# Output operands of the next token group split one tile per step, first norm in half-row steps

## The chip, the cores and the metric

The kernel runs on one core of one Trainium2 chip. The metric is the device time of one execution in microseconds (us), as the median of three runs. The engines are TensorE (PE in the profile), VectorE (DVE), ScalarE (ACT), GpSimd (POOL) and SyncE (SP), which issues the DMA transfers.

## The reference, cut to what matters

One layer of a decoder trunk on 2048 tokens of width 1024, in float32. One projection feeds two groups of heads, four recurrent ones (hgrn) and eight of stick-breaking attention. Their outputs are normalised, projected, normalised again and added to the residual; then come a feed-forward block (FFN) and a gated embedding.

```python
u = rmsnorm(h, attn_pre_norm[i])
proj = u @ w_in[i]
hq, hf, hi, hg, sq, sk, sv = jnp.split(proj, splits, axis=-1)
o_hg = rmsnorm(hgrn2_mix(hq, hf, hi, lb), hg_out_norm[i]) * silu(hg)
o_sb = rmsnorm(stick_breaking_mix(sq, sk, sv), sb_out_norm[i])
mix = jnp.concatenate([o_hg, o_sb], axis=-1) @ w_out[i]
h = h + rmsnorm(mix, attn_post_norm[i])
u = rmsnorm(h, ffn_pre_norm[i])
gate, up = jnp.split(u @ w_gate_up[i], [D_FF], axis=-1)
h = h + rmsnorm((silu(gate) * up) @ w_down[i], ffn_post_norm[i])
...
```

The change concerns `mix` (the output projection), the two norms behind it, and what is prepared for them.

## The kernel before, in words

**Tiling.** The 2048 tokens are cut into four groups of 512 (`NG`, `GT`), a group into four row blocks of 128 (`TT`), and the width of 1024 into eight blocks of 128 (`ND`); `HH` is 4, so tiles 0 to 3 of a group's output belong to the hgrn heads and tiles 4 to 7 to attention. Every product of two float32 tiles is made by three matmuls of a high and a low part (`mm3`, lines 217 to 219), so each operand is split first: ScalarE casts the high part (line 203), GpSimd or VectorE subtracts it for the low part (line 204). A weight is loaded and split in the same way by `weight`; of split weights three stand at a time.

**Stages.** In projection, attention and hgrn recurrence are woven together up to about 1144 us. Then the output projections of the four groups follow, `out_proj(0)` to `out_proj(3)`, at 1144 to 1244, 1244 to 1345, 1345 to 1405 and 1405 to 1460 us; attention and hgrn of the last group still run beside the first two. Behind them stand the FFN and the embedding, to 3011 us.

**What the change touches.** `out_load(g)` loads the eight output tiles of a group from `o_s` (line 627, tile `tmp`, two buffers), splits tiles 0 to 3 by lines 203 and 204, scales and splits tiles 4 to 7 by lines 631 (ScalarE) and 632 (VectorE), and sums the squares of the latter in `oss` (lines 636 and 638 on ScalarE, 639 on GpSimd). The split operands are called `uh` and `ul`; their pool holds two groups (`UB`). `out_proj(g)` first turns `oss` into the row scales `rg` (lines 653 to 656), then runs four quarters of the output columns, each in two parts, with the results in `mix` (lines 682 and 684). `post_mix(g)` is run beside the following `out_proj`: for each row block `t` it loads the residual `h`, computes the scale of the row (`row_rstd`: a sum of squares on ScalarE, line 267, and two small GpSimd instructions, lines 269 and 272), multiplies `mix` (line 708, VectorE, two halves), adds it to `h` (line 709, first half on VectorE, second half on GpSimd), computes the scale of the new row and writes the normalised row `un_s` (line 713, ScalarE).

**What sets the order.** `weave(main, slots, subs)` steps the main stream and deals out the steps of the others in proportion; `Stream` wraps a generator, `drain` runs it to its end. PE runs in the order in which the program is written. On VectorE, ScalarE, GpSimd and SyncE a scheduler with a time model of its own puts the instructions in order while the program is built, starting from the order in which they are written; on the chip each engine then runs its own list strictly in that order. The VectorE and GpSimd lists hold attention's work too: line 458 is the low part of an attention operand, line 441 its scan, line 445 a product behind the scan, line 572 a product of the recurrence. `t_first` and `turn` prepare the FFN's first operands (lines 822 and 823: `uh`, `wh`, `wl` of a tile `wr`).

In the program before, `out_load(g + 1)` is written in one piece ahead of `out_proj(g)` (for the last group, ahead of `out_proj(2)`; for group 0, ahead of the last projection stretch, `n == 6`), and `post_mix` yields once for each row block.

## Time and profile before

| | us |
|---|---|
| median of three runs | 3013.46 (3012.3, 3013.46, 3015.99) |
| the profiled execution | 3012.98 |
| its span on the core | 3010.8 |
| PE busy | 2915.9 (97%) |
| VectorE busy | 2088.6 (69%) |
| ScalarE busy | 1576.9 (52%) |
| GpSimd busy | 1437.9 (48%) |
| out_proj(0) to out_proj(3) | 1144 to 1460 |

The profile comes from one execution; the span runs from its first to its last record. The shares are means over stages that differ much. Beside them the trace has, for any stretch of the span, the busy time of each engine and the granted TensorE clock as a share of full speed, the list of an engine's instructions in time, and the idle times of an engine with what ended them. In a row of a timeline the bracket gives the idle time ahead of the instruction and the instruction that released it.

### The profile page before, as it was taken

How to read it: one execution, taken by the hardware profiler on the slowest of the kernel's cores; microseconds unless marked ns; L12 is line 12 of the kernel's file. 1: busy time of each engine (PE TensorE's matmuls, PEld its weight loads, DVE VectorE, ACT ScalarE, POOL GpSimd, SP SyncE). 2: the span in 40 equal slices, each digit the busy share in tenths (PEclk: the TensorE clock that was granted, in tenths of full speed). 3: DMA queues.
4: the chain of work that ended last, by engine and by line, in shares of the span. 5: the costliest groups of instructions: out<-in, count | busy, mean ns of one | idle time of the engine just before them, and what ended most of it. 6: DMA issues, size and time to landing. Idle time of an engine off the chain costs nothing. (4 is left out here: it accounts for less than half of the span.)

```text
span 3010.8 us, 52896 instructions
## 1 busy us (share of the span) xinstructions
PE 2915.9 (97%) x18316; PEld 2423.5 (80%) x18316; DVE 2088.6 (69%) x2953; ACT 1576.9 (52%) x3180; POOL 1437.9 (48%) x1398
## 2 busy tenths in 40 slices
PE   8999999999999999898899999999999999999999
PEld 7888788878787888788777778888888888878777
DVE  3555666677777776756788787755787776656685
ACT  5666756666667666667523233445433323545542
POOL 3344455545556666855523222445723231446653
PEclk9999999999999999999999999999999999999999
DMA  7775665455445444557867677667965555677974
GB/s 220 217 215 152 180 181 164 146 171 164 139 138 163 148 132 140 162 182 268 277 219 246 222 263 244 213 191 224 334 204 168 175 173 174 207 217 226 333 249 160
DMA packets 469419, 602.28 MB, mean 200 GB/s; under 512 B 43168, under 2 KB 277664, under 8 KB 469152
## 3 DMA queue, kind: packets, MB, share of 16 engines
q1 hardware_dynamic: 469152, 598.91, 63.6%
q8 instruction: 144, 2.36, 0.3%
q14 instruction: 123, 1.01, 0.1%
HBM read 439.89 MB, written 158.86 MB: 199 GB/s over the span
## 5 line engine op out<-in xcount | busy, mean ns | idle before, releaser
L822 ACT CAST wh<-wr 128x512 fp32r<-128x512 f32 x600 | 351.8, 618 | 459.4 <-PE mm L218 187.2
L823 POOL TENSOR_TENSOR wl<-wr,wh 128x512 fp32r<-128x512 f32 x256 | 372.3, 1460 | 453.0 <-ACT wh L822 426.7
L445 POOL TENSOR_TENSOR a<-be,ring 128x512 f32<-128x512 f32 (+2 forms) x320 | 318.8, 997 | 415.2 <-DVE ring L441 390.1
L217 PE MATMUL mm<-uh,wh 128*128 128x512 f32 x1168 | 484.4, 415 | 7.2 <-DVE c L830 2.2
L219 PE MATMUL mm<-uh,wl 128*128 128x512 f32 x1168 | 460.7, 394 | 2.3 <-DVE wl L823 2.3
L218 PE MATMUL mm<-ul,wh 128*128 128x512 f32 x1168 | 459.2, 393 | 0.0
L823 DVE TENSOR_TENSOR wl<-wr,wh 128x512 fp32r<-128x512 f32 x344 | 297.7, 873 | 167.4 <-ACT wh L822 160.7
L441 DVE TENSOR_TENSOR_SCAN ring<-z,ring,be 128x512 f32<-128x512 f32 x192 | 245.7, 1280 | 105.5 <-ACT z L427 102.5
L217 PE MATMUL mm<-wh,uh 128*128 128x256 f32 (+1 forms) x992 | 306.5, 309 | 0.1
L218 PE MATMUL mm<-wl,uh 128*128 128x256 f32 (+1 forms) x992 | 291.6, 294 | 0.8 <-POOL wl L823 0.8
L219 PE MATMUL mm<-wh,ul 128*128 128x256 f32 (+1 forms) x992 | 291.6, 294 | 0.0
L219 PEld LDWEIGHTS mm<-uh,wl 128*128 128x128 f32 x1168 | 220.4, 189 | 53.5 <-DVE wl L823 2.7
L217 PEld LDWEIGHTS mm<-uh,wh 128*128 128x128 f32 x1168 | 221.6, 190 | 51.3 <-issue 3.3
L218 PEld LDWEIGHTS mm<-ul,wh 128*128 128x128 f32 x1168 | 221.7, 190 | 39.9 <-DVE ul L823 0.5
L458 DVE TENSOR_TENSOR al<-tr,ah 128x512 fp32r<-128x512 f32 (+1 forms) x320 | 192.1, 600 | 84.5 <-ACT ah L456 83.8
L203 ACT CAST wh<-wr 128x512 fp32r<-128x512 f32 x288 | 178.1, 619 | 132.7 <-PE mm L218 75.0
L204 POOL TENSOR_TENSOR wl<-wr,wh 128x512 fp32r<-128x512 f32 x144 | 190.1, 1320 | 102.8 <-ACT wh L203 92.1
L823 POOL TENSOR_TENSOR wl<-s,wh 128x512 fp32r<-128x512 f32 x44 | 95.5, 2175 | 274.0 <-ACT wh L822 255.5
L456 ACT CAST ah<-tr 128x512 fp32r<-128x512 f32 (+1 forms) x320 | 167.7, 524 | 106.4 <-PE tr L453 102.8
L426 ACT ACTIVATE be<-z 128x512 f32<-128x512 f32 (+2 forms) x320 | 171.1, 535 | 87.0 <-PE z L424 36.9
L217 PEld LDWEIGHTS mm<-wh,uh 128*128 128x128 f32 x992 | 189.5, 191 | 8.1 <-issue 0.3
L218 PEld LDWEIGHTS mm<-wl,uh 128*128 128x128 f32 x992 | 189.8, 191 | 6.3 <-POOL wl L823 1.2
(317 smaller groups left out, 7261.8 us busy)
## 6 DMA issues: line engine op xcount, KB each, us to landing
wr<-in_w_gate_up_dram SPq DMA_DIRECT2D x308, 256.0 KB, 3.9
wr<-in_w_in_dram SPq DMA_DIRECT2D x224, 256.0 KB, 3.1
wr<-hid_s SPq DMA_DIRECT2D x154, 256.0 KB, 3.0
wr<-in_w_down_dram SPq DMA_DIRECT2D x110, 256.0 KB, 3.4
wr<-wd_s SPq DMA_DIRECT2D x88, 256.0 KB, 3.2
kt<-k_s SPq DMA_DIRECT2D x80, 256.0 KB, 3.1
vt<-v_s SPq DMA_DIRECT2D x80, 256.0 KB, 3.3
wr<-h_s SPq DMA_DIRECT2D x80, 256.0 KB, 4.1
```

What stands on the lines that cost most here:

```text
L203: nc.scalar.copy(hi, src)
L204: (lo_engine or nc.gpsimd).tensor_tensor(lo, src, hi.bitcast(F32), op=ALU.subtract)
L217: nc.tensor.matmul(o, l[0], r[0], start=start, stop=False)
L218: nc.tensor.matmul(o, l[0], r[1], start=False, stop=False)
L219: nc.tensor.matmul(o, l[1], r[0], start=False, stop=stop)
L426: nc.scalar.activation(be[:, :n], z[:, :n], AF.Sigmoid, scale=0.125)
L441: nc.vector.tensor_tensor_scan(r[:, o:o + n][:, ::-1], z[:, :n][:, ::-1], be[:, :n][:, ::-1], init, op0=ALU.mult, op1=ALU.bypass)
L445: nc.gpsimd.tensor_tensor(a[:, :n], be[:, :n], r[:, o + 1:o + n + 1], op=ALU.mult)
L456: nc.scalar.copy(hi[:, lo_c:], tr[:, lo_c:])
L458: nc.vector.tensor_tensor(lo[:, lo_c:], tr[:, lo_c:], hi[:, lo_c:].bitcast(F32), op=ALU.subtract)
L822: nc.scalar.copy(hi, src)
L823: lo_engine.tensor_tensor(lo, src, hi.bitcast(F32), op=ALU.subtract)
```

## The change

`out_load` becomes a generator of nine steps: the first loads tile 0, each further one loads the next tile and splits the one at hand. It is dealt out over the slots of the preceding stream: for group 0 over the second half of the last projection stretch, for group 1 over `out_proj(0)`, for groups 2 and 3 over `out_proj(1)` and `out_proj(2)`. `post_mix` becomes eight steps of half a row: the loads and the first scale of a row (`ready`) are written one row ahead, the normalised row (`normed`) one step late. No arithmetic is changed and no instruction is added or taken away.

```diff
--- before.py
+++ after.py
@@ -619,12 +619,20 @@
     HG_STEPS = HH * 11 + 2
 
 
+    def o_raw(g, i):
+        r = tmp()
+        nc.sync.dma_start(r, o_s[g][i])
+        return r
+
     def out_load(g, res):
+
         ops = []
         acc = None
+        nxt = o_raw(g, 0)
+        yield
         for i in range(ND):
-            raw = tmp()
-            nc.sync.dma_start(raw, o_s[g][i])
+            raw = nxt
+            nxt = o_raw(g, i + 1) if i + 1 < ND else None
             if i >= HH:
                 hi, lo = operand(wpool, "u", UB)
                 gs = g_sb[:, i - HH:i - HH + 1]
@@ -639,7 +647,9 @@
                     nc.gpsimd.tensor_tensor(acc, acc, raw, op=ALU.add)
             else:
                 ops.append(split(wpool, "u", UB, raw))
-        res["o"], res["oss"] = ops, acc
+            if i == ND - 1:
+                res["o"], res["oss"] = ops, acc
+            yield
 
     def out_proj(g, res):
         ops, acc = res["o"], res["oss"]
@@ -698,21 +708,36 @@
         gb = [xt("gb") for _ in range(2)]
         for j in range(2):
             nc.sync.dma_start(gb[j], attn_post_norm[0:1][:, j * GT:(j + 1) * GT].to_broadcast((P, GT)))
-        for t in range(TT):
+
+        def ready(t):
             hs = [xt("h"), xt("h")]
             for j in range(2):
                 nc.sync.dma_start(hs[j], x[g * GT + t * P:g * GT + (t + 1) * P, j * GT:(j + 1) * GT])
-            r = row_rstd(mix[t])
+            return hs, row_rstd(mix[t])
+
+        def normed(t, hs, r):
+            for j in range(2):
+                nc.scalar.activation(mix[t][j], hs[j], AF.Copy, scale=r)
+                nc.sync.dma_start(un_s[g][t * P:(t + 1) * P, j * GT:(j + 1) * GT], mix[t][j])
+
+        nxt = ready(0)
+        late = None
+        for t in range(TT):
+            hs, r = nxt
             for j in range(2):
                 d = mix[t][j]
                 nc.vector.scalar_tensor_tensor(d, d, r, gb[j], op0=ALU.mult, op1=ALU.mult)
                 (nc.gpsimd if j else nc.vector).tensor_tensor(hs[j], hs[j], d, op=ALU.add)
                 nc.sync.dma_start(h_s[g][t * P:(t + 1) * P, j * GT:(j + 1) * GT], hs[j])
-            r = row_rstd(hs)
-            for j in range(2):
-                nc.scalar.activation(mix[t][j], hs[j], AF.Copy, scale=r)
-                nc.sync.dma_start(un_s[g][t * P:(t + 1) * P, j * GT:(j + 1) * GT], mix[t][j])
-            yield
+                if j == 0:
+                    if late is not None:
+                        normed(*late)
+                else:
+                    nxt = ready(t + 1) if t + 1 < TT else None
+                    late = (t, hs, row_rstd(hs))
+                    if t + 1 == TT:
+                        normed(*late)
+                yield
 
     def post_late(g):
 
@@ -1239,8 +1264,14 @@
         nxt = g + 2 if kind == "b" and g + 2 < NG else None
         toks = in_norm(nxt) if nxt else []
         if n == 6:
-            out_load(0, res[0])
-        weave(main, slots - tail, ra.part(slots - tail), rh.part(slots - tail, 1 if hg_n < slots else None))
+            ol = Stream(out_load(0, res[0]))
+        if n == 6:
+            part = slots // 2
+            weave(main, slots - part, ra.part(slots - part), rh.part(slots - part, 1 if hg_n < slots else None))
+            weave(main, part, ra.part(part), rh.part(part, 1 if hg_n < slots else None), (ol, ND + 1, 0))
+            ol.drain()
+        else:
+            weave(main, slots - tail, ra.part(slots - tail), rh.part(slots - tail, 1 if hg_n < slots else None))
         if n in (3, 5):
             hg.drain()
         if nxt:
@@ -1263,26 +1294,25 @@
                 yield
 
     for g in range(NG - 1):
-        if g + 1 < NG - 1:
-            out_load(g + 1, res[g + 1])
+        ol = Stream(out_load(g + 1, res[g + 1]))
         op = Stream(out_proj(g, res[g]))
         if g == 0:
             weave(op, 2, rates.part(2), r2.part(2))
             hgs[2].drain()
-            weave(op, OP_SLOTS - 2, rates.part(OP_SLOTS - 2), r3.part(OP_SLOTS - 2))
+            weave(op, OP_SLOTS - 2, rates.part(OP_SLOTS - 2), r3.part(OP_SLOTS - 2), (ol, ND + 1, 0))
         elif g == 1:
-            weave(op, half, rates.part(half), r3.part(half), (pm, TT, 0))
+            weave(op, half, rates.part(half), r3.part(half), (pm, 2 * TT, 0), (ol, 4, 1))
             tu = Stream(turn(un_s[0], u_s[0], g_ffn, ["mm"], xt, ev))
-            weave(op, half, rates.part(half), r3.part(half), (tu, 9, 0))
+            weave(op, half, rates.part(half), r3.part(half), (tu, 9, 0), (ol, 5, 1))
             hgs[3].drain()
             att_stream.drain()
             side.close()
             big[0] = ctx.enter_context(tc.tile_pool(name="bigr", bufs=1, side="right"))
             mm_tags[:] = ["mm", "z", "mm", "z", "mm", "av"]
         else:
-            out_load(NG - 1, res[NG - 1])
-            weave(op, half, (pm, TT, 0))
+            weave(op, half, (pm, 2 * TT, 0), (ol, ND + 1, 1))
             weave(op, half, (Stream(first_operands()), ND, 1))
+        ol.drain()
         op.drain()
         pm = Stream(post_mix(g, res[g]["mix"]))
 
@@ -1291,7 +1321,7 @@
     drive.prepare(2)
     op = Stream(out_proj(NG - 1, res[NG - 1]))
     tu = Stream(turn(un_s[1], u_s[1], g_ffn, ["tr", "hg"], xt, ev))
-    weave(op, half + 2, (pm, TT, 0), (tu, 9, 0))
+    weave(op, half + 2, (pm, 2 * TT, 0), (tu, 9, 0))
 
     def third_operands():
         for k in range(ND // 2):
```

PE's list is the same in both programs. The other lists move less than the diff suggests, since the scheduler had already spread the burst: tiles 0 to 5 of each `out_load` stand about where they stood. Two places where the lists differ follow, on two engines each. The numbers behind names count tiles in the program and differ from before to after.

**VectorE, early in out_proj(1).** `mix`, `rstd2`, `gb` and `h` belong to `post_mix(0)`, `ul<-tmp` is a tile of group 2's operands, `al` an attention operand. Before:

```order
L441 SCALAR_TENSOR_TENSOR ring3_204<-z_16649,be_16653 128x512
L653 COPY rg_18230<-hgss_181 128x4
L632 SCALAR_TENSOR_TENSOR ul_16636<-tmp_16633,g_sb_572,uh_16635 128x512
L458 TENSOR_TENSOR al_16669<-tr_16662,ah_16667 128x512
L632 SCALAR_TENSOR_TENSOR ul_16644<-tmp_16641,g_sb_572,uh_16643 128x512
L654 COPY rg_16721<-tr_16716 128x4
L608 TENSOR_TENSOR gate_16040<-hg_16552,gate_16040 128x512
L708 SCALAR_TENSOR_TENSOR mix_15294<-mix_15294,rstd2_16935,gb_16684 128x512
L708 SCALAR_TENSOR_TENSOR mix_15948<-mix_15948,rstd2_16935,gb_16685 128x512
```

After:

```order
L441 SCALAR_TENSOR_TENSOR ring3_204<-z_16593,be_16597 128x512
L729 SCALAR_TENSOR_TENSOR mix_15238<-mix_15238,rstd2_16803,gb_16628 128x512
L729 SCALAR_TENSOR_TENSOR mix_15918<-mix_15918,rstd2_16803,gb_16629 128x512
L730 TENSOR_TENSOR h_16794<-h_16794,mix_15238 128x512
L458 TENSOR_TENSOR al_16613<-tr_16606,ah_16611 128x512
L664 COPY rg_16651<-tr_16646 128x4
L608 TENSOR_TENSOR gate_16010<-hg_16552,gate_16010 128x512
L729 SCALAR_TENSOR_TENSOR mix_15239<-mix_15239,rstd2_17001,gb_16628 128x512
L729 SCALAR_TENSOR_TENSOR mix_15919<-mix_15919,rstd2_17001,gb_16629 128x512
L730 TENSOR_TENSOR h_16992<-h_16992,mix_15239 128x512
```

The two operand tiles (line 632, now line 640) are gone from here, and rows 1 and 2 of the norm (line 729, formerly 708) stand on both sides of `al`.

**GpSimd, behind that.** `qp` is the recurrence's product for which PE waits, `rg` the row scales of `out_proj(1)`. Before:

```order
L655 TENSOR_SCALAR rg_16721<-rg_16721 128x8
L639 TENSOR_TENSOR oss_16623<-oss_16623,tmp_16641 128x512
L709 TENSOR_TENSOR h_16927<-h_16927,mix_15948 128x512
L656 TENSOR_TENSOR rg_16721<-rg_16721,neghalf_168 128x8
L445 TENSOR_TENSOR a_16766<-be_16762,ring0_198 128x512
L572 TENSOR_TENSOR qp_16778<-qp_16778,pd_16776 128x256
```

After:

```order
L665 TENSOR_SCALAR rg_16651<-rg_16651 128x8
L269 TENSOR_SCALAR ssum_17006<-ss_17003 128x1
L269 TENSOR_SCALAR ssum_17195<-ss_17192 128x1
L730 TENSOR_TENSOR h_16993<-h_16993,mix_15919 128x512
L666 TENSOR_TENSOR rg_16651<-rg_16651,neghalf_168 128x8
L272 TENSOR_TENSOR rstd2_17008<-ssum_17006,neghalf_168 128x1
L272 TENSOR_TENSOR rstd2_17197<-ssum_17195,neghalf_168 128x1
L445 TENSOR_TENSOR a_16696<-be_16692,ring0_198 128x512
L572 TENSOR_TENSOR qp_16708<-qp_16708,pd_16706 128x256
```

The operand tile (line 639) has left, and the scales of further rows (lines 269 and 272) stand ahead of `qp`.

**ScalarE, in out_proj(2).** `wh<-wr` by line 203 is a weight of the output projection, `uh<-wr` by line 822 (now 847) an FFN operand, `junk` a sum of squares. Before:

```order
L203 CAST wh_18429<-wr_18427 128x512
L822 CAST uh_18618<-wr_18616 128x512
L822 CAST uh_18651<-wr_18649 128x512
L267 ACTIVATE junk_191,ss_18322<-h_18305 128x512
L822 CAST uh_18696<-wr_18694 128x512
L822 CAST uh_18729<-wr_18727 128x512
L682 ACTIVATE mix_18238<-mm_18278,rg_18230 128x256
L631 ACTIVATE uh_18187<-tmp_18185,g_sb_572 128x512
L267 ACTIVATE junk_191,ss_18322<-h_18306 128x512
L203 CAST wh_18435<-wr_18433 128x512
```

After:

```order
L203 CAST wh_18385<-wr_18383 128x512
L847 CAST uh_18651<-wr_18649 128x512
L267 ACTIVATE junk_191,ss_18437<-mix_16659 128x512
L847 CAST uh_18696<-wr_18694 128x512
L847 CAST uh_18729<-wr_18727 128x512
L847 CAST uh_18774<-wr_18772 128x512
L720 ACTIVATE mix_16657<-h_18219,rstd2_18341 128x512
L720 ACTIVATE mix_17492<-h_18220,rstd2_18341 128x512
L847 CAST uh_18807<-wr_18805 128x512
L203 CAST wh_18391<-wr_18389 128x512
```

Between the two weights stand five FFN operands and a normalised row (line 720) now, where four FFN operands, an evacuation (line 682) and an operand tile (line 631) stood.

**GpSimd, a little later in out_proj(2).** Before:

```order
L204 TENSOR_TENSOR wl_18436<-wr_18433,wh_18435 128x512
L639 TENSOR_TENSOR oss_18167<-oss_18167,tmp_18185 128x512
L269 TENSOR_SCALAR ssum_18406<-ss_18403 128x1
L272 TENSOR_TENSOR rstd2_18408<-ssum_18406,neghalf_168 128x1
L709 TENSOR_TENSOR h_18400<-h_18400,mix_17529 128x512
L204 TENSOR_TENSOR wl_18530<-wr_18527,wh_18529 128x512
```

After:

```order
L204 TENSOR_TENSOR wl_18392<-wr_18389,wh_18391 128x512
L269 TENSOR_SCALAR ssum_18440<-ss_18437 128x1
L272 TENSOR_TENSOR rstd2_18442<-ssum_18440,neghalf_168 128x1
L647 TENSOR_TENSOR oss_18414<-oss_18414,tmp_18408 128x512
L730 TENSOR_TENSOR h_18434<-h_18434,mix_17494 128x512
L269 TENSOR_SCALAR ssum_18447<-ss_18444 128x1
L848 TENSOR_TENSOR wl_18908<-wr_18903,wh_18907 128x512
L204 TENSOR_TENSOR wl_18502<-wr_18499,wh_18501 128x512
```

The norm's add of row 3 (line 730) and one FFN split (line 848) have come ahead of the weight's low part `wl_18502` (before, `wl_18530`).

## Rows read from the trace of the kernel before

**Rows 1.** The page's first part: busy time of each engine over the span.

```profile
PE 2915.9 (97%) x18316; PEld 2423.5 (80%) x18316; DVE 2088.6 (69%) x2953; ACT 1576.9 (52%) x3180; POOL 1437.9 (48%) x1398
```

**Rows 2.** Waits of PE, 929 to 960 us: place, total us, times, longest.

```profile
PE hg L535 <- POOL qp L572: 0.8, 1, 0.8
```

**Rows 3.** Waits of PE, 1144 to 1244 us.

```profile
PE av L470 <- DVE al L458: 4.8, 1, 4.8
```

**Rows 4.** Waits of PE, 1244 to 1345 us.

```profile
PE hg L535 <- POOL qp L572: 5.1, 3, 2.6
PE av L470 <- DVE al L458: 2.3, 1, 2.3
...
PE hg L535 <- DVE small L538: 1.1, 1, 1.1
PE av L469 <- ACT ah L456: 1.0, 1, 1.0
```

**Rows 5.** Waits of PE, 1345 to 1405 us.

```profile
PE z L218 <- POOL wl L204: 8.4, 4, 4.2
```

**Rows 6.** Waits of PE, 1405 to 1460 us.

```profile
PE z L218 <- POOL wl L204: 0.9, 2, 0.5
```

**Rows 7.** Windows: span, busy (count) PE, PEld, DVE, ACT, POOL, clock, DMA share, GB/s.

```profile
1091.00:1105.00 14.00, 14.00 (x137) 11.53 (x136) 9.83 (x15) 9.78 (x23) 11.86 (x17) 1.00 0.58 189
...
1197.00:1207.00 10.00, 10.00 (x161) 8.70 (x160) 6.65 (x10) 6.72 (x14) 5.71 (x11) 1.00 0.44 135
...
1244.00:1268.00 24.00, 17.81 (x272) 15.71 (x272) 18.10 (x25) 15.46 (x36) 22.68 (x25) 0.99 0.64 205
...
1238.00:1245.00 7.00, 5.52 (x27) 5.34 (x27) 5.25 (x8) 4.80 (x12) 6.00 (x11) 0.52 0.42 151
1275.00:1282.00 7.00, 4.95 (x34) 4.52 (x35) 5.63 (x7) 3.46 (x12) 4.99 (x6) 0.53 0.54 187
1357.00:1364.00 7.00, 3.54 (x16) 3.54 (x17) 6.43 (x7) 4.84 (x11) 6.19 (x5) 0.52 1.02 339
```

**Rows 8.** Instructions on the tile tmp: form, count, min/median/max ns.

```profile
L632 DVE SCALAR_TENSOR_TENSOR ul<-tmp,g_sb,uh x16: 724/751/1783, 939.4 to 1365.2; 128x512 fp32r<-128x512 f32 x16
...
L639 POOL TENSOR_TENSOR oss<-oss,tmp x12: 1258/1304/1749, 946.2 to 1367.8; 128x512 f32<-128x512 f32 x12
```

**Rows 9.** Instructions of line 708: min/median/max ns.

```profile
L708 DVE SCALAR_TENSOR_TENSOR mix<-mix,rstd,gb x24: 737/752/1779, 1233.6 to 1434.2; 128x512 f32<-128x512 f32 x24
```

**Rows 10.** Timeline of VectorE, 1231.5 to 1241 us: start, us, instruction [idle <- releaser].

```profile
1233.57 2.77 DVE L708 SCALAR_TENSOR_TENSOR mix<-mix,rstd,gb 128x512 f32<-128x512 f32 x2 [0.47 <-POOL rstd L272]
1236.26 0.88 DVE L632 SCALAR_TENSOR_TENSOR ul<-tmp,g_sb,uh 128x512 fp32r<-128x512 f32 x1
...
1238.75 0.68 DVE L458 TENSOR_TENSOR al<-tr,ah 128x512 fp32r<-128x512 f32 x1
```

**Rows 11.** Timeline of GpSimd, 1247 to 1268 us.

```profile
1254.20 1.84 POOL L656 TENSOR_TENSOR rg<-rg,neghalf 128x8 f32<-128x8 f32 x1
...
1257.07 0.83 POOL L572 TENSOR_TENSOR qp<-qp,pd 128x256 f32<-128x256 f32 x1
...
1260.87 1.01 POOL L272 TENSOR_TENSOR rstd<-ssum,neghalf 128x1 f32<-128x1 f32 x1
```

**Rows 12.** Timeline of VectorE, 1272 to 1279 us.

```profile
1273.58 2.62 DVE L708 SCALAR_TENSOR_TENSOR mix<-mix,rstd,gb 128x512 f32<-128x512 f32 x2
```

**Rows 13.** Timeline of ScalarE, 1349 to 1370 us.

```profile
1357.13 1.15 ACT L822 CAST uh<-wr 128x512 fp32r<-128x512 f32 x2
...
1365.13 0.62 ACT L203 CAST wh<-wr 128x512 fp32r<-128x512 f32 x1 [3.04 <-PE mm L219]
```

**Rows 14.** Timeline of GpSimd, 1345 to 1392 us.

```profile
1357.08 1.65 POOL L709 TENSOR_TENSOR h<-h,mix 128x512 f32<-128x512 f32 x1 [1.29 <-DVE mix L708]
...
1372.25 1.68 POOL L709 TENSOR_TENSOR h<-h,mix 128x512 f32<-128x512 f32 x1 [1.60 <-DVE mix L708]
...
1375.56 3.45 POOL L823 TENSOR_TENSOR wl<-wr,wh 128x512 fp32r<-128x512 f32 x2
```

## The prediction

> **What bounds the kernel now.** I read the share of busy time first: PE is busy for 2915.9 of 3010.8 us, and the next engine, VectorE, for 69% of the span [rows 1]. So PE sets the time, its list is the same in both programs, and the change can only move PE's idle time and the clock that it is granted. All of PE's idle time is about 95 us (3010.8 less 2915.9). Next I read the list of PE's waits, stretch by stretch, where the moved instructions stand. Around the end of the projections there is one wait of 0.8 us, for GpSimd [rows 2]; beside out_proj(0) and (1) attention waits 4.8 us for one low part `al` and later 2.3, and the recurrence 5.1 us in three pieces for `qp` [rows 3, 4]; in out_proj(2) PE waits four times, 8.4 us together, for the low part of a weight [rows 5]; in out_proj(3) 0.9 us [rows 6]. That is 22.3 us, with smaller ones of 1.1 and 1.0 [rows 4] some 24 us, and it is all that this change can reach directly. Third come the windows: in three of seven microseconds each, at 1238, 1275 and 1357 us, the granted clock is 0.52 or 0.53, the lower of the two levels [rows 7]. Each stands right behind one of the long waits (the 4.8 us for the `al` of 1238.75 [rows 10], the 2.3 us for the next late one, and the longest of the four for weights, 4.2 us). In the three, PE is busy for 5.52, 4.95 and 3.54 us; at full clock the same matmuls would take half, so a slow stretch costs 2.8, 2.5 and 1.8 us. Direct waits and slow stretches together: about 31 us, 1% of the time. A gain above that is excluded.
>
> **The change part by part.** The sum is made against the profiled execution, 3012.98 us, which lies 0.5 under the median of 3013.46.
>
> *Operand tiles.* Comparing the lists, tiles 0 to 5 of each group stay about where they were. Tiles 6 and 7 (per group two loads, five ScalarE, two VectorE and three GpSimd instructions, GpSimd's `oss` add of tile 5 among them) go to a later place. One VectorE instruction is 0.75 us, one GpSimd add 1.30 [rows 8], so 1.5 and 3.9 us of work leave one place and come to another.
>
> - Group 0: they leave 945 to 959 us, where a 0.8 us wait of PE [rows 2] stands with GpSimd's add next to it, and come to 1091 to 1105, where PE is busy for all of 14.00 us, and GpSimd for 11.86 [rows 7]. There 2.1 us of GpSimd are free, 1.8 less than the 3.9 that come; out_proj(0) needs them only at 1144, so the cover is the rest of that stretch. I take -0.7; without the cover, up to +1.8.
> - Group 1 goes to 1197 to 1207, where PE never waits and GpSimd is busy for 5.71 of 10.00 us [rows 7]: room for 3.9. One `qp` can come 0.8 late behind one add. I take +0.4, from 0 to 1.3. It leaves 1145 to 1160, where it cost PE nothing that the waits show.
> - Group 2 leaves the start of out_proj(1), told below, and group 3 leaves out_proj(2), below too; at 1309 to 1318 and 1372 to 1385, where they come to, the projection of their own group is still 20 us and more away. Zero, from -1 to 2.
>
> *Start of out_proj(1).* The 4.8 us wait [rows 3] is for the `al` of 1238.75 [rows 10]. Ahead of it VectorE runs line 708 twice for 2.77 us, behind the row scale, and then an operand tile for 0.88 us [rows 10]. In the new list tiles 4 and 5 and row 0's line 729 still stand ahead of that `al`: it stays, and its slow stretch with it. Bounds: 1.6 us less if the tiles come sooner, 2 more if the row scale comes later.
>
> *Behind it.* Rows 1 to 3 of the norm come earlier; before, row 2 stands at 1273.58 with 2.62 us [rows 12] and stands just ahead of the `al` of the 2.3 us wait. In the new list rows 1 and 2 are done sooner, so these 2.3 and the 1.0 behind them [rows 4] go: -3.3. Against it, GpSimd is busy for 22.68 of 24.00 us from 1244 to 1268 [rows 7]; `qp` stands behind the 1.84 us power of line 656 [rows 11]. One `oss` add of 1.30 leaves the queue ahead of it, and the add of a further row (1.68, as in [rows 14]) and three pairs of lines 269 and 272 come: the second of a pair ranges up to 1.01 [rows 11]. Add for add that is 0.4 later, and the pairs bring up to 1.0 each, some of it in gaps that the queue has anyway: I take 2 us later in all, +2.0 on the 5.1 of the waits for `qp`. The slow stretch at 1275 costs 2.5 and follows the waits that go; I give it an even chance of going too: -1.2. Sum of this place: -2.5. Bounds: all four kinds of wait and the slow stretch gone, -12; nothing gone and all three pairs at 1.0 with 0.4 each time, +4.
>
> *out_proj(2).* Here ScalarE and GpSimd decide, since each weight waits for its cast and then its low part. The longest wait, 4.2 us [rows 5], ends with a low part that stands behind GpSimd's add at 1357.08, which itself waits 1.29 us for VectorE's line 708 [rows 14]. The row comes earlier now: about 2.6 us of that wait go, but the next weight's cast, at 1365.13, waits 3.04 us for PE to free its buffer [rows 13]. In the new list five FFN casts, two by two at 1.15 us [rows 13], and a normalised row stand between the second and third weight's casts on ScalarE, so I let the third low part come no earlier than before, and all 2.6 are given back. For the fourth, one FFN split (3.45 for two, so 1.7) and the last row's add (1.68) now stand ahead, and an add and its 1.60 us wait [rows 14] go: between 0 and 3.4, and I take +2.0, its middle and a little, since the FFN split is surely there and the wait is not surely gone. Bounds of the place: all 8.4 us and the slow stretch gone, less 10; both engines' extra work in full behind the slow stretch, +8.
>
> *out_proj(3).* Two adds of the norm (1.68 each) stand ahead of low parts where one stood; the waits there are 0.9 us in two pieces [rows 6]. I take +1.0, from -1 to 3.3.
>
> Sum: -0.7 + 0.4 + 0 - 2.5 + 2.0 + 1.0 = +0.2, so 3013.2 for an execution like the profiled one, and 3013.7 as a median. What a measurement of this kernel can tell from no change is about 0.2%, 6 us.
>
> **The rivals.**
>
> *The bursts dissolve (faster).* If the waits at the places named are less a matter of the order than of the heap of work, they shorten together. The start of out_proj(1) would give back 2.0 of 4.8 and its slow stretch 2.8; the place behind it 3.3 and 2.5, less 2.0; out_proj(2) 2.6 and 1.8; group 0 gives 0.7. Together -13.7, so 2999.8 as a median. For it: all three slow stretches follow waits [rows 3 to 5, 7], and an end to one wait gains twice. Against it: at the first wait the same work stands ahead of the same `al`.
>
> *ScalarE's and GpSimd's queues in out_proj(2) (slower).* The price is the work that comes ahead of the weights: two FFN casts more than PE waits for (1.2), the normalised row (1.3, as two halves), 3.4 on GpSimd, and 3.3 in out_proj(3), 9.2 us; the slow stretch lasts one time more, 1.8: 11.0, with the gain of the place before it cancelled by its `qp` chain, so 3024.5. It decides once the FFN tiles, whose DMA share is at 1.02 in that window [rows 7], land later than ScalarE reaches their casts: from then on each cast holds the weight behind it.
>
> *The shared read path (a little slower).* Line 708 has a median of 0.75 us and a maximum of 1.78 [rows 9]; the pair at 1233.57 takes 2.77 and that at 1273.58 takes 2.62, beside a busy GpSimd [rows 10, 12]. If the denser rows make all six pairs that moved take 1.2 us more, and half of it lies on the path, 3.6 us come on top: 3017.3, still within 0.2%. The Trainium skill, "SBUF — State Buffer", section "Who interferes with whom", says that a VectorE instruction with two inputs in SBUF and a GpSimd instruction that reads SBUF exclude each other, and that the one issued first holds the shared read interface throughout. By that rule this rival would be the likely case wherever both queues are full; these rows agree with it, but line 708 was slowed there already, so they show no added cost.
>
> *The change doesn't do what it says.* The scheduler leaves three quarters of the tiles where they were; this is in the forecast already, as the term of zero.
>
> **How the numbers follow.** The forecast (3013.7, its own range 3009 to 3018) gets 0.40; the dissolving bursts 0.27; the queues in out_proj(2) 0.20; the shared path 0.06; 0.07 is left for what I do not see, 0.03 of it faster and 0.04 slower. Faster by over 0.2%: 0.27 + 0.03 = 0.30. Within: 0.40 + 0.06 = 0.46. Slower: 0.20 + 0.04 = 0.24. The range reaches a little past both rivals' times, since each has more than 0.2 and their bounds (-12 and +8 at the two decisive places) are wide: 2998 to 3026.
>
> **What would show it.** In the profile after: a wait of PE for `al` of 4 to 5 us at about 1239 with a clock near 0.5 behind it (first step); no wait for `al` of over 1 us between 1268 and 1290, and waits for `qp` of 6 to 8 us together (second); waits for weights in out_proj(2) of 9 to 12 us, the third and fourth the longest (third). The sum is wrong if the slow stretches do not follow the waits, if the first `al` comes early, or if something changes behind 1460 us, where the lists differ only by swaps of a place or two.

## The result, and the profile after

The changed kernel takes 3021.03 us (median of 15 runs, 3015.93 to 3024.77) beside 3013.34 us for the kernel before (15 runs): a ratio of 1.0025 with a 95% interval of 1.0018 to 1.0032. In a second comparison, below, it is 1.0018 (1.0007 to 1.0028). So the change makes the kernel slower by about 0.2%, 5 to 8 us. The forecast was 3013.7, no change that can be measured; the range held the result, and the sign was that of the slower rival.

The profiled execution of the changed kernel is one of its longest, 3024.74 us with a span of 3022.5. Its share of busy time, to be read against [rows 1]:

```profile
PE 2924.0 (97%) x18316; PEld 2433.4 (81%) x18316; DVE 2089.4 (69%) x2953; ACT 1574.4 (52%) x3180; POOL 1430.8 (47%) x1398
```

PE is busy for 8.1 us longer with the same list of matmuls. Over the whole trace the granted clock is 0.990 instead of 0.993, and busy time times clock is 2895 us in both (2915.9 x 0.993, 2924.0 x 0.990), so the lower clock accounts for the 8.1; the rest of the 11.7 us by which the span grew is waiting. The lists of PE's waits, in the stretches of [rows 3 to 6] (the last one ten us longer, since the work has moved back by then); first out_proj(0):

```profile
PE av L470 <- DVE al L458: 5.0, 1, 5.0
```

out_proj(1):

```profile
PE hg L535 <- POOL qp L572: 6.2, 2, 4.2
...
PE hg L546 <- POOL qp L572: 1.5, 2, 1.2
PE tr L661 <- DVE al L458: 0.7, 1, 0.7
PE av L470 <- DVE al L458: 0.3, 1, 0.3
```

out_proj(2):

```profile
PE z L218 <- POOL wl L204: 8.7, 3, 4.4
```

out_proj(3):

```profile
PE z L218 <- POOL wl L204: 5.0, 2, 3.2
PE av L217 <- ACT wh L203: 2.0, 1, 2.0
PE av L218 <- POOL wl L204: 0.9, 1, 0.9
PE tr L782 <- DVE rg L664: 0.4, 1, 0.4
```

Three of the four stretches came out near the forecast: the 5 us for the first `al` stayed, the later `al` fell from 2.3 to 0.3, the waits for `qp` rose from 5.1 to 7.7 (6.2 by line 535 and 1.5 by line 546). The weights of out_proj(2) stayed at 8 to 9, where 9 to 12 had been named. The fourth did not: the waits for GpSimd's low parts in out_proj(3) rose from 0.9 [rows 6] to 5.0 us.

Since PE's list is the same, the start of one and the same matmul can be compared in both traces, and the difference says how much has been lost up to there. Two matmuls that bracket out_proj(3), in PE's timeline before (start, duration, instruction, idle time before it and its releaser):

```profile
1415.18 0.38 PE L218 MATMUL z<-wl,uh 128*128 128x256 f32 x1 [0.43 <-POOL wl L204]
...
1449.39 0.38 PE L217 MATMUL av<-wh,uh 128*128 128x256 f32 x1 [1.63 <-ACT wh L203]
```

The same two, and one between them, in the timeline after:

```profile
1419.54 0.38 PE L218 MATMUL z<-wl,uh 128*128 128x256 f32 x1 [1.77 <-POOL wl L204]
...
1431.19 0.58 PE L218 MATMUL z<-wl,uh 128*128 128x256 f32 x1 [3.24 <-POOL wl L204]
...
1460.70 0.41 PE L217 MATMUL av<-wh,uh 128*128 128x256 f32 x1 [2.03 <-ACT wh L203]
```

The first is late by 4.4 us (1419.54 - 1415.18), the second by 11.3. Windows of the kernel after show what came on top of the waits, here with four of the earlier stretches (columns as in [rows 7]; the clock is the third number from the end):

```profile
1240.00:1245.00 5.00, 2.73 (x12) 2.55 (x13) 5.00 (x8) 3.74 (x10) 4.38 (x9) 0.50 0.55 174
1265.00:1275.00 10.00, 7.85 (x97) 7.20 (x98) 4.33 (x9) 3.87 (x10) 6.08 (x9) 0.66 0.68 227
1362.00:1369.00 7.00, 7.00 (x48) 7.00 (x48) 6.08 (x12) 7.00 (x15) 4.07 (x4) 0.76 0.99 348
1376.00:1383.00 7.00, 3.85 (x20) 3.85 (x21) 3.90 (x5) 4.39 (x9) 6.09 (x7) 0.76 1.02 368
1419.00:1426.00 7.00, 6.46 (x41) 6.46 (x42) 3.78 (x6) 6.09 (x15) 2.78 (x5) 0.76 0.94 301
1426.00:1433.00 7.00, 3.76 (x25) 3.55 (x24) 2.80 (x6) 3.33 (x8) 3.85 (x4) 0.80 1.00 345
1433.00:1440.00 7.00, 7.00 (x46) 7.00 (x45) 0.00 (x0) 3.98 (x9) 2.01 (x2) 0.71 0.92 342
1461.00:1468.00 7.00, 6.07 (x29) 5.96 (x29) 6.11 (x8) 2.52 (x6) 0.99 (x1) 0.52 1.07 349
```

Before, the clock of out_proj(3) was full (1.00 over 1405 to 1460). Now three stretches of seven us have 0.76, 0.80 and 0.71. With PE busy for 6.46, 3.76 and 7.00 us in them, that costs 6.46 x 0.24 + 3.76 x 0.20 + 7.00 x 0.29 = 4.3 us. A fourth, at 1461, has 0.52, behind the wait of 2.03 us; the matmuls that ended out_proj(3) at 1460 before run until 1474 now, so it belongs to this stretch too and costs another 6.07 x 0.48 = 2.9. The waits of the stretch went from 4.3 us (with the 1.6 and two smaller ones of 1.0 and 0.8 beside [rows 6]) to 8.3, 4.0 more. Together that is 11.2 us, an estimate from these windows, beside the 10.6 that the stretch lost by the table below: more of it is clock than waiting.

The queue that made it, GpSimd's after (out_proj(3)):

```profile
1415.44 1.28 POOL L730 TENSOR_TENSOR h<-h,mix 128x512 f32<-128x512 f32 x1
...
1418.22 1.26 POOL L204 TENSOR_TENSOR wl<-wr,wh 128x512 fp32r<-128x512 f32 x1
...
1428.14 1.77 POOL L730 TENSOR_TENSOR h<-h,mix 128x512 f32<-128x512 f32 x1 [3.10 <-DMA un_s<-mix]
1429.88 1.26 POOL L204 TENSOR_TENSOR wl<-wr,wh 128x512 fp32r<-128x512 f32 x1
```

VectorE's, and the loads of the residual on SyncE:

```profile
1425.39 0.69 DVE L730 TENSOR_TENSOR h<-h,mix 128x512 f32<-128x512 f32 x1 [2.56 <-DMA h<-in_x_dram]
```

```profile
1420.91 1.31 SPq L715 DMA_DIRECT2D h<-in_x_dram  x2
...
1430.75 1.00 SPq L715 DMA_DIRECT2D h<-in_x_dram  x2
```

The norm's second add (1415.44) stands ahead of one low part (`wl` at 1418.22), its third (1428.14) ahead of the next (1429.88). The third had been waiting for 3.10 us. The two halves of its `h` were loaded at 1420.91 only, and VectorE's half of the row waited 2.56 us for its load. What ended the wait of GpSimd's half is not shown: its row names a store, which is an inference. That the late loads hold it is tested by E6.

### The profile page after: what moved, and what is told of

Same layout as the page of the kernel before. It is cut to its first block, busy times and chain, and to the rows that moved or that the text cites. A ratio compares the mean times of both kernels' runs of the same rounds, so it can differ in the third digit from the quotient of the medians.

```text
span 3022.5 us, 52906 instructions
## 1 busy us (share of the span) xinstructions
PE 2924.0 (97%) x18316; PEld 2433.4 (81%) x18316; DVE 2089.4 (69%) x2953; ACT 1574.4 (52%) x3180; POOL 1430.8 (47%) x1398
## 5 line engine op out<-in xcount | busy, mean ns | idle before, releaser
L848 DVE TENSOR_TENSOR wl<-wr,wh 128x512 fp32r<-128x512 f32 x344 | 305.1, 895 | 172.2 <-ACT wh L847 161.8
L441 DVE TENSOR_TENSOR_SCAN ring<-z,ring,be 128x512 f32<-128x512 f32 x192 | 245.6, 1279 | 104.9 <-ACT z L427 101.7
```

Source lines behind the costliest of these rows:

```text
L441: nc.vector.tensor_tensor_scan(r[:, o:o + n][:, ::-1], z[:, :n][:, ::-1], be[:, :n][:, ::-1], init, op0=ALU.mult, op1=ALU.bypass)
L848: lo_engine.tensor_tensor(lo, src, hi.bitcast(F32), op=ALU.subtract)
```

## The experiments

Each kernel was run in several rounds beside the kernel before on the same chip. The ratio is not formed from the two medians, so it can differ a little from their quotient. E5 to E8 ran on another chip, where the kernel before took 3016.53 us; their expectations, in us, were made from some 3013, so they are compared by the ratio here.

| kernel | median, us | before, us | ratio (95%) |
|---|---|---|---|
| the change, first comparison | 3021.03 | 3013.34 | 1.0025 (1.0018 to 1.0032) |
| E1 the change again | 3017.50 | 3012.11 | 1.0018 (1.0007 to 1.0028) |
| E2 tiles alone | 3007.55 | 3012.11 | 0.9984 (0.9973 to 0.9996) |
| E3 norm alone | 3023.27 | 3012.11 | 1.0032 (1.0020 to 1.0045) |
| E4 norm beside out_proj(3) as before | 3012.84 | 3012.11 | 0.9998 (0.9987 to 1.0010) |
| E5 its adds on VectorE | 3017.37 | 3016.53 | 1.0006 (0.9997 to 1.0015) |
| E6 turn's inputs in another ring | 3013.46 | 3016.53 | 0.9991 (0.9982 to 1.0000) |
| E7 norm beside out_proj(1) as before | 3017.77 | 3016.53 | 0.9998 (0.9988 to 1.0008) |
| E8 old norm, tiles of groups 0 to 2 | 3008.41 | 3016.53 | 0.9973 (0.9963 to 0.9982) |
| E9 old norm, tiles of group 2 | 3003.91 | 3012.60 | 0.9974 (0.9963 to 0.9984) |
| E10 E9 and turn's inputs in another ring | 3003.60 | 3012.60 | 0.9967 (0.9956 to 0.9979) |
| E11 old norm, tiles of group 0 | 3008.05 | 3012.60 | 0.9988 (0.9979 to 0.9997) |
| E12 adds beside out_proj(1) on VectorE | 3020.78 | 3012.60 | 1.0026 (1.0015 to 1.0037) |

The next table gives, from one trace of each, how much later (+) or earlier (-) than in the kernel before the same matmul starts at the end of a stretch than at its beginning (times of before, us):

| kernel | 400-960 | 960-1144 | 1144-1244 | 1244-1290 | 1290-1345 | 1345-1405 | 1405-1460 |
|---|---|---|---|---|---|---|---|
| the change | -0.5 | +3.0 | +1.0 | -1.9 | +1.8 | +1.2 | +10.6 |
| E1 | -1.0 | +1.1 | +1.1 | -1.9 | +0.7 | +2.1 | +9.7 |
| E2 | -0.6 | +1.9 | -1.5 | -7.7 | +1.6 | +1.8 | +2.1 |
| E3 | +1.3 | +1.1 | -1.4 | +1.1 | 0.0 | +3.5 | +5.9 |
| E4 | -0.7 | +2.0 | +1.5 | -3.4 | +1.2 | +2.4 | +3.1 |
| E5 | -0.2 | +2.9 | +0.7 | -3.4 | +1.0 | +2.3 | +3.0 |
| E6 | -0.2 | +2.7 | +1.2 | -3.4 | +1.6 | +2.0 | +0.9 |
| E7 | -0.4 | +2.8 | -0.4 | -6.0 | +1.6 | +3.3 | +7.9 |
| E8 | -0.5 | +3.1 | -1.3 | -7.4 | +1.1 | +2.4 | +2.8 |
| E9 | +1.1 | +2.5 | -2.5 | -8.2 | +0.7 | +1.0 | +0.1 |
| E10 | +0.7 | +1.2 | -3.1 | -5.4 | +1.2 | +1.2 | +0.3 |
| E11 | -0.4 | +0.4 | +0.8 | -3.8 | -0.2 | +0.1 | +2.4 |
| E12 | -0.6 | +3.7 | +0.5 | -2.8 | +1.4 | +3.0 | +10.7 |

The first two lines are two executions of one kernel; they differ by up to 2 us in a stretch shown, and by 5 in the stages behind 1460 us. E9 and E10, whose lists are the same up to 1345 us, differ by 2.8 between 1244 and 1290. So a difference of 3 us in this table says nothing alone; one of 6, or a smaller one that many kernels show alike, does.

**E1, the change again.**

> The changed kernel once more, unaltered, to see how much of its loss is steady and whether the same places carry it. Theory one (the norm's half-row steps beside out_proj(3): the residual loads of rows 2 and 3 wait for a buffer of the ring of eight that they share with turn's inputs, the adds on GpSimd wait for them, and weights stand behind the adds): 3021, with waits for a weight's low part of about 5 us in 1405 to 1470 and a granted clock under 1 behind them. Rival one (the moved operand tiles): 3021 too, with the loss in the recurrence's qp waits. Rival two (no place of its own, only a slower clock in some executions): the places differ from those of the first profile.

The place is the same: out_proj(3) loses 9.7 us. The waits in 1405 to 1470:

```profile
PE z L218 <- POOL wl L204: 4.7, 3, 1.9
```

4.7 us where 5 were expected. The time is 3.5 us under the 3021 expected, a ratio of 1.0018 instead of 1.0025. The rival that puts the loss into the waits for `qp` does not fit, since 9.7 us are lost where there are none; the rival without a place falls.

**E2 and E3, each half of the change alone.** E2 is the changed kernel with `post_mix` of the kernel before and `(pm, TT, 0)` in the weaves; E3 is the kernel before with the new `post_mix` and these lines:

```diff
-            weave(op, half, rates.part(half), r3.part(half), (pm, TT, 0))
+            weave(op, half, rates.part(half), r3.part(half), (pm, 2 * TT, 0))
...
-            weave(op, half, (pm, TT, 0))
+            weave(op, half, (pm, 2 * TT, 0))
...
-    weave(op, half + 2, (pm, TT, 0), (tu, 9, 0))
+    weave(op, half + 2, (pm, 2 * TT, 0), (tu, 9, 0))
```

> Only the operand tiles are dealt out one per step; the norm keeps its whole-row steps. Theory one: no loss, 3009 to 3015, and the waits for weights in out_proj(3) are under 2 us as before. Rival one: 3019 to 3023, the whole loss. Rival two: anything, with a wide spread.

> Only the norm's half-row steps; the operand tiles are written in one piece as before. Theory one: 3018 to 3023, with waits for a low part of 4 to 5 us in out_proj(3). Rival one: 3011 to 3015.

The two halves pull against each other: the tiles alone make the kernel faster by 0.16%, the norm alone slower by 0.32%. Theory one expected the tiles to be neutral, 3009 to 3015; they take 3007.55 and gain 7.7 us in 1244 to 1290, which it had no place for. The norm alone is at the upper end of its 3018 to 3023 (3023.27); it loses 5.9 us in out_proj(3), with 3.8 us of waits for low parts there instead of 4 to 5, and 3.5 in out_proj(2). The waits of E2 from 1144 to 1244 and from 1244 to 1290, to be read against [rows 3, 4]:

```profile
PE av L470 <- DVE al L458: 3.1, 1, 3.1
```

```profile
PE hg L535 <- POOL qp L572: 1.9, 1, 1.9
```

3.1 instead of 4.8 for the first `al`, 1.9 instead of 5.1 for `qp` (with 1.0 more by line 546), and none for the later `al`. Why the first `al` comes earlier stands in VectorE's timelines. Before, between the lines of [rows 10]:

```profile
1237.07 0.86 DVE L684 SCALAR_TENSOR_TENSOR mix<-mm,rg,mix 128x256 f32<-128x256 f32 x2
1237.85 0.97 DVE L709 TENSOR_TENSOR h<-h,mix 128x512 f32<-128x512 f32 x1
```

E2:

```profile
1235.94 0.88 DVE L640 SCALAR_TENSOR_TENSOR ul<-tmp,g_sb,uh 128x512 fp32r<-128x512 f32 x1
1236.75 0.68 DVE L458 TENSOR_TENSOR al<-tr,ah 128x512 fp32r<-128x512 f32 x1
```

Before, the results of out_proj(0) (`mix<-mm`) and row 0's add stand between the operand tile and `al`; in E2 they stand behind `al`. It is so in all traces: with the old norm beside out_proj(1) and group 2's tiles dealt out (E2, E7 to E10) `al` stands right behind the tile and the wait is 2.9 to 3.4 us; in the others the two stand ahead and it is 4.5 to 5.1.

**E4, the norm beside out_proj(3) as before.** `post_mix(2)` in whole rows, everything else as changed.

```diff
-        pm = Stream(post_mix(g, res[g]["mix"]))
+        pm = Stream((post_mix_row if g in (2,) else post_mix)(g, res[g]["mix"]))
...
-    weave(op, half + 2, (pm, 2 * TT, 0), (tu, 9, 0))
+    weave(op, half + 2, (pm, TT, 0), (tu, 9, 0))
```

> The changed kernel, but post_mix(2), which runs beside out_proj(3), in the old whole-row steps. Theory one: the 8.5 us that the first profile lost between 1410 and 1455 come back, 3011 to 3015. Rival one: 3021 still. Rival two: 3021 still, or a spread without a place.

3012.84, inside theory one's bounds: the loss is gone, and out_proj(3) stands at +3.1 instead of about +10. So the norm's half-row steps at this one place carry the loss. Its GpSimd timeline, and the load of row 2 on SyncE's:

```profile
1427.10 1.28 POOL L204 TENSOR_TENSOR wl<-wr,wh 128x512 fp32r<-128x512 f32 x1 [1.59 <-ACT wh L203]
1428.43 1.66 POOL L719 TENSOR_TENSOR h<-h,mix 128x512 f32<-128x512 f32 x1
```

```profile
1421.80 0.90 SPq L714 DMA_DIRECT2D h<-in_x_dram  x2
```

Row 2 is loaded no earlier with the old norm (1421.80 beside 1420.91), and its add starts at about the same time (1428.43 beside 1428.14). But here the add stands behind the weight's low part, in the changed kernel ahead of it. How much each of the two counts, the next two ask.

**E5, the adds off GpSimd; E6, the loads made early.** E5:

```diff
-                (nc.gpsimd if j else nc.vector).tensor_tensor(hs[j], hs[j], d, op=ALU.add)
+                (nc.gpsimd if j and g < 2 else nc.vector).tensor_tensor(hs[j], hs[j], d, op=ALU.add)
```

E6:

```diff
-    tu = Stream(turn(un_s[1], u_s[1], g_ffn, ["tr", "hg"], xt, ev))
+    tu = Stream(turn(un_s[1], u_s[1], g_ffn, ["tr", "hg"], lambda: slot("wr", 0, "wr"), ev))
```

> The changed kernel, but the second half of each of post_mix(2)'s adds runs on VectorE instead of GpSimd, so that no add stands ahead of a weight's low part in GpSimd's queue; the half-row steps and the load times stay. If the place of the adds in GpSimd's queue is the cause of the loss beside out_proj(3): the waits there for a low part from GpSimd fall from 4 to 5 us to about 1, the granted clock stays at full speed, and 7 of the 8 us that the kernel with the old norm at this place had gained are gained here too: 3011 to 3015. If the late loads of the residual are the cause, VectorE waits for them in the same way and holds its own low parts: 3016 to 3020.

> The changed kernel, but turn's inputs beside out_proj(3) lie in the ring of the FFN's weight tiles instead of the ring of eight that the residual rows use, so rows 2 and 3 of the residual can be loaded earlier; the adds stay ahead of the low parts on GpSimd. If the late loads are the cause: the second wait for a low part, 1.9 to 3.2 us, falls under 1 and the time to 3011 to 3016. If the place in the queue alone decides: one add of 1.3 us still stands ahead of each low part, 3016 to 3021.

Waits of PE in 1405 to 1470 of E5, then of E6:

```profile
PE z L218 <- POOL wl L204: 2.0, 2, 1.2
```

```profile
PE z L218 <- POOL wl L204: 2.6, 2, 1.8
```

Either edit halves the waits for low parts, and the stretch's loss falls from about 10 to 3.0 and 0.9 us. By the time, E5's 1.0006 lies between its two expectations, and its interval overlaps that of E1, so its gain is not clear by the time alone. E6's 0.9991 is as fast as the late loads had it, or a little faster. In E5 the clock is 1.00 up to 1454 only, not throughout as the first expectation had it; the next window costs 6.67 x 0.24 = 1.6 of the 3.0 us:

```profile
1454.00:1461.00 7.00, 6.67 (x43) 6.68 (x44) 5.40 (x8) 3.89 (x8) 1.17 (x2) 0.76 1.08 358
```

The loads of the residual on SyncE's timeline of E6:

```profile
1384.05 1.02 SPq L715 DMA_DIRECT2D h<-in_x_dram  x2
...
1420.21 0.49 SPq L715 DMA_DIRECT2D h<-in_x_dram  x1
...
1424.13 0.42 SPq L715 DMA_DIRECT2D h<-in_x_dram  x1
```

The two halves of row 2 are loaded at 1384.05 now, where they were at 1420.91; row 3's at 1420.21 and 1424.13 instead of 1430.75. GpSimd's timeline of E6:

```profile
1414.51 1.28 POOL L730 TENSOR_TENSOR h<-h,mix 128x512 f32<-128x512 f32 x1
...
1417.29 1.27 POOL L204 TENSOR_TENSOR wl<-wr,wh 128x512 fp32r<-128x512 f32 x1
1419.85 1.67 POOL L730 TENSOR_TENSOR h<-h,mix 128x512 f32<-128x512 f32 x1 [1.29 <-DVE mix L729]
...
1426.02 1.86 POOL L204 TENSOR_TENSOR wl<-wr,wh 128x512 fp32r<-128x512 f32 x1 [2.10 <-ACT wh L203]
```

Row 2's add is at 1419.85, 6 us before its low part, which waits for its own cast. Row 1's (1414.51) still stands ahead of the low part at 1417.29, and that wait of 1.8 us stays. And the clock, over the same time as in the kernel after:

```profile
1419.00:1426.00 7.00, 5.62 (x48) 5.42 (x48) 5.90 (x10) 5.27 (x14) 3.71 (x5) 1.00 0.78 253
1426.00:1433.00 7.00, 6.14 (x53) 5.94 (x52) 2.11 (x3) 6.35 (x15) 5.28 (x6) 1.00 0.99 339
```

It is full throughout, up to 1475 us. So the cause has two parts that both must be there: the adds come to stand ahead of low parts, and their loads come late. The loads cannot come earlier because one ring of eight tiles has to serve two rows of residual (four tiles), the two gains `gb` and turn's inputs (two tiles in use and two loaded ahead), ten in all. The third row then waits for the first to be done. The program loads a row ahead; the ring does not let it. All kernels with both parts (the change, E1, E3, E7, E12) lose 5.9 to 10.7 us in this stretch, all others 0.1 to 3.1.

**E7, the norm beside out_proj(1) as before.** As E4, with `g in (0,)`.

> The changed kernel, but post_mix(0), beside out_proj(1), in the old whole-row steps. If the early rows of the norm take back there what the operand tiles' leaving had given (the kernel with the tiles alone gained 7.7 us between 1244 and 1290, the changed one 1.9): 5 to 6 us under the changed kernel, 3012 to 3016, and the waits for qp in that stretch are about 2 us instead of 6. If the gain of the tiles alone was chance: 3017 to 3021.

1244 to 1290 gives 6.0 us instead of 1.9, and the time falls to that of the kernel before (0.9998), in the expected bounds by the ratio, 2 us over them in us. The waits for `qp` by line 535 are gone, 0.9 by line 546 remain, and the wait for the first `al` is 3.4. So the norm's half rows take back at out_proj(1) about 4 us of what the tiles give.

**E8 and E9, which tiles.** Both with the old norm. E8 deals out the tiles of groups 0 to 2 (`out_load_burst` is the old `out_load`), E9 of group 2 alone:

```diff
-        if g + 1 < NG - 1:
-            out_load(g + 1, res[g + 1])
+        ol = idle
+        if g == 0:
+            out_load_burst(g + 1, res[g + 1])
+        elif g == 1:
+            ol = Stream(out_load(g + 1, res[g + 1]))
...
-            weave(op, half, rates.part(half), r3.part(half), (pm, TT, 0))
+            weave(op, half, rates.part(half), r3.part(half), (pm, TT, 0), (ol, 4, 1))
...
-            weave(op, half, rates.part(half), r3.part(half), (tu, 9, 0))
+            weave(op, half, rates.part(half), r3.part(half), (tu, 9, 0), (ol, 5, 1))
```

> The old norm everywhere, the operand tiles one per step for groups 0, 1 and 2, and those of group 3 in one piece as before. If the moved tiles of group 3 cost out_proj(2) what the kernel with the tiles alone lost there and in out_proj(3) (1.8 and 2.1 us) while those of group 2 give the 7.7 us: 3002 to 3006, faster than both kernels by over 0.2%. If the tiles of group 3 have no part in it: 3007 to 3009, as the kernel with the tiles alone.

> The kernel before with one edit: only group 2's operand tiles are dealt out one per step, beside out_proj(1). If their leaving the start of out_proj(1) is the whole of the gain that the kernels with dealt-out tiles and the old norm had (7.4 and 7.7 us between 1244 and 1290, 0.16 and 0.27% in all): 7 to 8 us under the kernel before (0.23 to 0.27%), all of it in that stretch, and nothing lost between 960 and 1144, where the others lost 2 to 3. If the other groups' tiles are needed for it: within 3 us of before.

E8's ratio, 0.9973, is that of the first of its expectations (its us, on the other chip, that of the second). But it does not differ clearly from E2's 0.9984, and out_proj(2) and (3) show the same in both traces (+2.4 and +2.8 beside +1.8 and +2.1), so nothing shows that group 3's tiles cost anything.

E9 is as fast as E8, 0.26% under the kernel before, and has it all between 1144 and 1290 (-2.5 and -8.2). Between 1244 and 1290 it waits 1.2 us for an `al` and 1.9 for `qp` (1.0 by line 535, 0.9 by line 546), where the kernel before waits 2.3 and 5.1 [rows 4]. So group 2's two late tiles, ahead of attention's operands at the start of out_proj(1), are the part of the change that pays. One expectation failed: 960 to 1144 was to lose nothing in E9, and it shows +2.5 as the others do, though every engine's list is that of the kernel before up to 1231 us. That column is therefore the luck of single traces, and no cost of group 0's tiles.

**E10, E9 with turn's inputs in the other ring.** The edit of E6 on E9.

> The same, and turn's inputs beside out_proj(3) in the ring of the FFN's weight tiles, so that the residual rows are loaded earlier there. If late loads cost time beside out_proj(3) with the old norm too: 1 to 3 us less than the kernel with group 2's tiles alone. If they cost only behind adds that stand ahead of the low parts, as in the changed kernel: the same time within 1 us.

3003.60 and 0.9967 beside 3003.91 and 0.9974: no difference that can be told. So with the old norm the late loads cost nothing that shows. In E9 one add, row 1's, stands close ahead of a low part; in E10, with the loads early, two do, and PE waits 3.2 us for these low parts instead of 1.1, but the clock stays full and the stretch comes out the same (+0.3 beside +0.1).

**E11, group 0's tiles alone.**

```diff
-            out_load(0, res[0])
-        weave(main, slots - tail, ra.part(slots - tail), rh.part(slots - tail, 1 if hg_n < slots else None))
+            ol = Stream(out_load(0, res[0]))
+            part = slots // 2
+            weave(main, slots - part, ra.part(slots - part), rh.part(slots - part, 1 if hg_n < slots else None))
+            weave(main, part, ra.part(part), rh.part(part, 1 if hg_n < slots else None), (ol, ND + 1, 0))
+            ol.drain()
+        else:
+            weave(main, slots - tail, ra.part(slots - tail), rh.part(slots - tail, 1 if hg_n < slots else None))
```

> The kernel before with only group 0's operand tiles dealt out over the second half of the last projection stretch. If tiles 6 and 7 in their new place cost what the other kernels lost between 960 and 1144 (1 to 3 us): that loss there, and 1 to 3 us over the kernel before, which this measurement cannot tell from no change. If the loss has nothing to do with them: 0 there.

0.9988, faster by 0.12%, which neither expected; 960 to 1144 shows +0.4, as the second has it. Most of the gain, -3.8 us, shows between 1244 and 1290, where nothing was edited; but the scheduler, which plans from the beginning on, has filled 33 places of VectorE's list there otherwise. So a part of every gain in that stretch may be such a by-product. This isn't settled.

**E12, the adds beside out_proj(1) on VectorE.** As E5, with `if j and g`.

> The changed kernel, but the second halves of post_mix(0)'s adds, beside out_proj(1), on VectorE instead of GpSimd. If the adds in GpSimd's queue make the two waits for qp (2.0 and 4.2 us): these fall to 2 together and the stretch from 1244 to 1290 gains 3 to 4 us. If the pairs of small instructions for the rows' scales or VectorE's own work make them: the waits stay at 4 to 6 us, or turn into waits for al.

```profile
PE av L470 <- DVE al L458: 2.6, 3, 1.9
PE hg L535 <- DVE ks L574: 1.3, 1, 1.3
```

```profile
1245.00:1250.00 5.00, 4.89 (x23) 4.60 (x23) 5.00 (x7) 3.27 (x8) 4.81 (x6) 0.50 0.66 231
1250.00:1255.00 5.00, 5.00 (x52) 4.29 (x51) 4.56 (x8) 3.92 (x11) 4.64 (x5) 0.51 0.83 284
```

The waits for `qp`, 6.2 us, are gone without GpSimd's adds, as the first expectation had it. But 2.6 us of waits for `al` and 1.3 for another VectorE product took their place, as the second had it, and a stretch at half clock lasts from 1245 to 1255. Only 0.9 us remain as a gain (-2.8 instead of -1.9), which single traces can't tell from none. The kernel is no faster (1.0026): the work costs as much in VectorE's queue here as in GpSimd's.

## Why the prediction was right and wrong, point by point

- **Group 0 (-0.7).** Every kernel with these tiles moved gains 0.2 to 1.0 us up to 960, those without lose 0.7 to 1.3. Right. The cost between 960 and 1144 that the first trace showed is not theirs (E9, E11).
- **The middle of out_proj(0) (+0.4).** +1.0 and +1.1 from 1144 to 1244. The waits for `qp` there go from 0.2 us to 2.0 in two pieces, and they are 2.0 or 2.1 in every kernel with group 1's tiles dealt out. Right in kind; by the waits it is over the bound of 1.3.
- **The new places of groups 2 and 3 (0).** From 1290 to 1345, where group 2's tiles come to, all eleven kernels with these tiles moved lose 0.7 to 1.8 us, the two without (E3, E11) nothing. So the term is about +1, inside its bounds; put at zero, it was a little too low. No cost of group 3's tiles shows (E8 beside E2).
- **Start of out_proj(1) (0).** The wait stayed, 5.0 us, with the clock at 0.50 behind it. Right for the whole change. The reason was only half so. The tiles and row 0 do stand ahead of `al`, but so do two more instructions, which the scheduler puts behind it as soon as the tiles are dealt out and the norm is the old one: the wait is 3.1 then (E2).
- **Behind it (-2.5).** -1.9 in both executions; `qp` at 7.7 us, in the 6 to 8 that were forecast; the later `al` gone. The slow stretch did not go, it moved up to 1265 to 1275 (0.66), so the -1.2 for it did not come. Right in size, with the wrong reason for the `al`: it was to go because the norm's rows come earlier. With the norm alone (E3) PE waits 2.8 us there for an `al`, at two places, and the stretch loses 1.1; with the tiles alone (E2) the wait goes and the stretch gains 7.7. Together they gain 1.9, so the parts don't add: the half rows keep 4 to 6 us of the tiles' gain from coming (E7 and E2 against the change). That this came near -2.5 is luck.
- **out_proj(2) (+2.0).** +1.2 and +2.1. Right in size, but not by its mechanism. The 2.0 us were to be waiting for the fourth low part. The waits for low parts have three pieces now, 8.7 us, and with the smaller ones for a cast (0.8 before, 0.5 after) the sum is 9.2 both before and after. What grew is the time at the lower clock: two windows with 0.76 now (PE busy for 7.00 and 3.85 us), one with 0.52 before (3.54 [rows 7]), some 2.6 us beside 1.7. And kernels with the old norm and the old order of group 3's tiles show +1.0 to +2.4 there too (E8, E9), so the change's own part can't be told from the chance of single traces.
- **out_proj(3) (+1.0, to 3.3).** +10.6 and +9.7. This is the step that failed. It counted the two adds that stand ahead of low parts, at 1.68 each, by their durations. The first of them, row 1's, did cost that: a wait of 1.8 us. The second, row 2's, was priced as if its inputs were there: its load cannot come before the ring of eight is free (E6), so PE's wait for the low part behind it is 3.2 us. And the sum had no term here for the clock behind the waits, some 7 us, more than the 4.0 us of added waiting. With the place in the queue or the late loads away, 0.9 to 3.0 us remain, which is the term as forecast.
- **The rivals.** The slower rival gave 3024.5, against 3021.03. It had the right kind of mechanism, queues in order in which work stands ahead of weights and a load holds both, and one more slow stretch; but it placed it in out_proj(2), on ScalarE and FFN casts, with only 3.3 of its 11 us in out_proj(3). The faster rival, waits and slow stretches that go together, is what E9 shows at out_proj(1): -8.2 there, 0.26% in all. The change has these tiles too, but the norm's half rows hold back most of that gain at out_proj(1) and cost some 10 us in out_proj(3). That the forecast of nearly no change stood for two large effects against each other was not seen.
- **The shared read path.** The rows of the norm's multiply, over 1225 to 1445 us, 24 each: before and after.

```profile
1225.00:1445.00 220.00, 24.82 (x24) 0.95 0.68 228
```

```profile
1225.00:1445.00 220.00, 27.69 (x24) 0.93 0.66 218
```

24.8 us became 27.7, 2.9 more on VectorE, and 29.7 in E1; the norm alone has 27.4 (E3), the tiles alone 21.7 (E2). So the denser rows were slowed, by 3 to 5 us against the kernel before; the rival's 7.2 were too many. The Trainium skill, "SBUF — State Buffer", section "Who interferes with whom", says that a VectorE instruction with two inputs in SBUF contends with a GpSimd instruction that reads SBUF; the traces agree in sign, and with the adds beside out_proj(1) off GpSimd (E12) the eight rows there take 9.4 us instead of 11.3. No run shows that it reached PE.

Open stays how much of the gain of E9 is the scheduler's by-product, and why the price of the clock differs so between stretches with much the same waits.

## What to carry to other kernels

Price a moved instruction not by its duration alone but by when its inputs arrive: ahead of something urgent in an in-order queue it carries its wait along. A load written one step ahead is early only if its ring has a free tile, so count the tiles that live at once, those of other streams in the same ring too. And take a change in two parts apart before judging it: here the tiles alone gain 0.16% (0.26% with group 2's only) and the norm alone loses 0.32%, and together they look like little.

## What was not expected of the hardware

In out_proj(3), waits that grew by 4.0 us together were followed by some 20 us at a mean granted clock of 0.71 to 0.80 and seven more at 0.52, where before it was 1.00; by the estimate above that costs some 7 us, more than the added waiting. In E6, with 2.6 us of waits for low parts, the clock stayed at 1.00 in the same place, although one wait of 1.8 us was as long as the first one here; in E5, with 2.0, it stayed at 1.00 up to 1454 and then fell to 0.76 for one window. What the clock does is not told by a single wait. At out_proj(1) waits for VectorE and the clock (0.50 over ten us in E12) took back most of what moving the adds off GpSimd had gained. In out_proj(3) a price for the waits that leaves the clock out is too low by half or more.
